# Six adaLN steps to a batch instead of four, from the 24th step on

## The chip, the core and the metric

One NeuronCore of a Trainium2 chip runs the whole program in one launch. The metric is device time in microseconds (us) of one execution; the kernel before was run three times. Engines are named as in the profile: PE (TensorE matmul), DVE (VectorE), ACT (ScalarE), POOL (GpSimd), SP (SyncE, which here issues nearly all loads). A profiled execution's times count from the start of its span.

## The reference

One decoder layer of width 2048 over 256 prompt tokens and 8 samples of 4 tokens (288 columns in all), in float32:

```python
mod = jax.nn.silu(c) @ w_ada + b_ada
sh1, sc1, g1, sh2, sc2, g2 = jnp.split(mod[:, None, :], 6, axis=-1)
h = layer_norm(x) * (1 + sc1) + sh1
z = (h @ w_in).astype(f32)
...
mix = jnp.concatenate([ya, yb], axis=-1).astype(x.dtype) @ w_out
x1 = layer_norm(ALPHA * x + g1 * mix, ln1_g, ln1_b)
h2 = layer_norm(x1) * (1 + sc2) + sh2
a, u = jnp.split(h2 @ w_up, 2, axis=-1)
...
ff = (jax.nn.gelu(conv, approximate=False) * u) @ w_down
x2 = layer_norm(ALPHA * x1 + g2 * ff, ln2_g, ln2_b)
```

Between z and mix lie an mLSTM of 4 heads (ya) and an HGRN2 of 8 heads (yb), both in chunks and with states that are returned. The change touches only when the product silu(c) @ w_ada ("adaLN", 2048 by 12288) is done; c has 9 rows (one for the prompt, eight for the samples).

## The kernel before

**Main products.** Activations stand as tiles of 128 features by 288 tokens. A weight "granule" is a tile of 128x1024 (512 KB): eight blocks of 128x128. SP loads it into `raw` (L220), ACT rounds it to `whi` (L229), DVE subtracts to `wlo` (L156); the activation is split in the same way. Per block PE runs three matmuls, hi by xh, hi by xl, lo by xh, so a granule is 24 matmuls. `raw` and `wlo` share NR=7 buffers, `whi` has NH=4; `granule()` asks for loads NQ=5 ahead, casts 3 ahead and subtractions 2 ahead. `project` takes two granules for one output tile in the PSUM pool "mm" and calls `slot()` after each.

**What fills the gaps.** `slot()` first runs one step of each background generator (`tick`), then adds `rate` to `credit` and calls `ada_batch`, then runs one step of each active generator (`mlstm`, `hgrn`, which use the PSUM pool "sd" of five buffers).

**adaLN.** w_ada is 192 steps of 512 KB. `ada_step(s)` first has SP issue the load of step s+6 (L306, NA=7 buffers `araw`), which waits until PE is done with step s-1; then PE multiplies `csp` (silu(c), 32 columns) by `araw[s]`, 8 matmuls of 128x256 into one PSUM tile `ad` (up to step 31 the tiles are narrower and the matmuls more). A unit is one such tile: seven small units, and then units of 16 steps, that end at steps 15, 31, 47, 63, 79, 95 and so on. When a unit ends, `ada_finish` transposes the tile on DVE (L345) and adds the bias into `mod`; a new unit that begins before that was ticked has the transpose issued first. There is one buffer "ad". In the start stage every other unit uses "sd" in its place; from the mixer on all use "ad" (`ad_tag`).

**What paces it.** In the start stage each granule's group adds 1 or 2 to `credit`; in the mixer `rate` is RATE=1.3 per slot. Before, four credits buy four steps. Steps 8 to 31 feed `h` (the first normalised activations), and `ad_stop` ends this pacing at step 172; the rest stands at fixed places in the tail.

**The entry of the mixer.** After the start's last slot SP issues the rest of the constants `cs`, the parameters `pks`, and the masks `lmf` (L579 to L582); `pks` is awaited by DVE for the HGRN bounds (`lbm`, `lbe`, `lb`).

Of the kernel before, what the change touches and what calls it, by code (L numbers as in the profile page):

```python
# [36 lines left out]
NR = 7  # L37
NQ = 5
NA = 7
BATCH = 4  # L40
NS = 4
RATE = 1.3
RA = 2
# [95 lines left out]
class K:  # L139
# [168 lines left out]

    def ada_batch(self):

        while self.credit >= BATCH:
            self.credit -= BATCH
            for _ in range(BATCH):
                self.ada_step()

    def ada_step(self):
# [1437 lines left out]
```

## Time and profile before

| | us |
|---|---|
| median of three runs | 1588.38 |
| lowest, highest | 1585.81, 1590.32 |
| the profiled execution | 1587.27 |
| its span | 1585.4 |
| PE busy in it | 1547.0 (98%) |
| DVE, ACT busy | 1033.2, 699.1 |

A line of a timeline gives start, duration (of a merged group), engine, source line, operation and shape; what stands in brackets is how long the engine was idle before it and what ended that. PEclk is TensorE's granted clock as a share of full speed, so 1.00 is 2.4 GHz and 0.50 is 1.2 GHz.

### The profile page before, as it was taken

To read this page: it belongs to the slowest core of one execution; us is meant where nothing else is said; L and a number is where in the kernel's file an instruction comes from. 1 tells how busy PE (TensorE), PEld (TensorE's weight loads), DVE (VectorE), ACT (ScalarE), POOL (GpSimd) and SP (SyncE) were. 2 spreads that over 40 slices of the span, in tenths; PEclk is the share of its full clock that TensorE was granted. 3 is DMA by queue.
4 is the path that set the end of the run, shared out by engine and by line. 5 is a ranking of instruction groups with operands and counts; after the bars stand their busy time and mean duration, and the time that the engine had idled before them with its cause. 6 is when DMAs were issued, how large, how long until landed. Compare 5 with 4: busy or idle time off the path is not lost.

```text
span 1585.4 us, 32088 instructions
## 1 busy us (share of the span) xinstructions
PE 1547.0 (98%) x12755; PEld 1456.8 (92%) x12755; DVE 1033.2 (65%) x2096; ACT 699.1 (44%) x1230; POOL 274.0 (17%) x429
## 2 busy tenths in 40 slices
PE   7999989999999989998999999999999999999998
PEld 5998988888888878886999999999999999999996
DVE  5766577878888788779755555455555555555554
ACT  4423234565656655335643433334343334444333
POOL 0000012344354343126311100011110001111000
PEclk9999999999999999999999999999999999999999
DMA  9998855777768678782555555555555555555551
GB/s 354 370 349 309 322 180 150 288 263 284 281 245 319 239 278 313 263 326 94 169 161 170 162 163 163 171 169 165 168 162 161 164 174 165 167 166 167 159 155 69
DMA packets 97542, 340.82 MB, mean 215 GB/s; under 512 B 11240, under 2 KB 15856, under 8 KB 96368
## 3 DMA queue, kind: packets, MB, share of 16 engines
q1 hardware_dynamic: 94896, 328.55, 60.8%
q0 software_dynamic: 2496, 10.22, 1.7%
q8 instruction: 101, 1.65, 0.4%
q14 instruction: 49, 0.40, 0.1%
HBM read 326.51 MB, written 12.21 MB: 214 GB/s over the span
## 4 chain that ended last, share of the span: by engine, by line
PE 86%; DVE 8%; ACT 3%; DMA 2%; issue 1%; SPq 0%; POOL 0%; ACTq 0%; DVEq 0%
PE mm L169 70%; PE sd L169 12%; PE ad L169 4%; DVE t L156 3%; DVE wlo L156 2%; ACT t L166 1%; DVE t L159 1%; ACT whi L229 1%; DVE c L159 1%; DMA raw<-w_in_b 1%; DMA raw<-w_out_b 0%; DMA pks<-pk 0%; DVE t L163 0%; DMA x<-xt 0%; ACT t L189 0%
## 5 line engine op out<-in xcount | busy, mean ns | idle before, releaser
L169 PE MATMUL mm<-t,whi 128*128 128x288 f32 (+1 forms) x4624 | 938.1, 298 | 14.0 <-ACT whi L229 5.8
L169 PEld LDWEIGHTS mm<-t,whi 128*128 128x128 f32 (+1 forms) x4624 | 741.6, 188 | 29.0 <-ACT whi L229 8.4
L169 PE MATMUL mm<-t,wlo 128*128 128x288 f32 x2312 | 683.4, 296 | 3.2 <-DVE wlo L156 3.2
L229 ACT CAST whi<-raw 128x1024 fp32r<-128x1024 f32 (+2 forms) x413 | 423.1, 1027 | 453.2 <-PE mm L169 223.8
L156 DVE TENSOR_TENSOR wlo<-raw,whi 128x1024 fp32r<-128x1024 f32 (+2 forms) x413 | 501.6, 1215 | 15.4 <-ACT whi L229 10.5
L169 PEld LDWEIGHTS mm<-t,wlo 128*128 128x128 f32 x2312 | 435.5, 188 | 4.1 <-DVE wlo L156 4.0
L169 PE MATMUL mm<-ff,whi 128*128 128x288 f32 x1376 | 276.1, 297 | 0.0
L169 PEld LDWEIGHTS mm<-ff,whi 128*128 128x128 f32 x1376 | 220.6, 188 | 2.5 <-issue 1.9
L166 ACT ACTIVATE t<-t 128x288 f32<-128x288 f32 (+4 forms) x317 | 121.5, 395 | 187.2 <-DVE t L156 130.4
L169 PE MATMUL mm<-ff,wlo 128*128 128x288 f32 x688 | 203.0, 295 | 0.0
L156 POOL TENSOR_TENSOR t<-t,t 128x288 f32<-128x288 f32 (+3 forms) x136 | 120.8, 896 | 168.6 <-ACT t L166 101.0
L159 DVE SCALAR_TENSOR_TENSOR t<-mm,mod,t 128x256 f32<-128x256 f32 x96 | 46.3, 482 | 148.1 <-PE mm L169 139.9
L169 PEld LDWEIGHTS mm<-ff,wlo 128*128 128x128 f32 x688 | 129.1, 188 | 0.0
L1558 POOL COPY convo<-ext 128x2 f32<-128x2 f32 x43 | 7.9, 184 | 629.4 <-ACT ext L1552 629.4
L156 DVE TENSOR_TENSOR t<-t,t 128x288 f32<-128x288 f32 (+4 forms) x203 | 89.8, 464 | 25.3 <-ACT t L189 21.2
L1553 DVE COPY ext<-mm 128x32 f32<-128x32 f32 x42 | 8.1, 192 | 138.8 <-ACT ext L1552 138.8
L169 PE MATMUL sd<-t,whi 128*128 128x288 f32 x464 | 95.0, 297 | 0.0
L169 PEld LDWEIGHTS sd<-t,whi 128*128 128x128 f32 x464 | 75.1, 190 | 0.0
L156 DVE TENSOR_TENSOR t<-cv,mm 128x256 f32<-128x256 f32 x80 | 20.7, 301 | 78.8 <-PE mm L169 78.8
L169 PE MATMUL ad<-araw,csp 128*32 128x256 f32 (+2 forms) x1312 | 68.4, 345 | 0.0
L169 PE MATMUL sd<-t,wlo 128*128 128x288 f32 x232 | 68.4, 296 | 0.0
L156 DVE TENSOR_TENSOR t<-t,mm 128x288 f32<-128x288 f32 x70 | 31.5, 451 | 54.5 <-PE mm L169 54.3
(259 smaller groups left out, 1206.8 us busy)
## 6 DMA issues: line engine op xcount, KB each, us to landing
araw<-w_ada SPq DMA_DIRECT2D x180, 512.0 KB, 5.7
raw<-w_up_b SPq DMA_DIRECT2D x160, 512.0 KB, 3.6
raw<-w_in_a SPq DMA_DIRECT2D x56, 512.0 KB, 7.3
raw<-w_in_b SPq DMA_DIRECT2D x56, 512.0 KB, 6.7
raw<-w_down SPq DMA_DIRECT2D x48, 512.0 KB, 3.5
raw<-w_down SPq DMA_DIRECT2D x32, 384.0 KB, 3.1
raw<-w_out_a SPq DMA_DIRECT2D x16, 512.0 KB, 6.2
raw<-w_out_b SPq DMA_DIRECT2D x16, 512.0 KB, 5.8
```

Of the source, the lines that this page charges most:

```text
L156: (eng or self.nc.vector).tensor_tensor(out=out, in0=a, in1=b, op=op)
L159: self.nc.vector.scalar_tensor_tensor(out=out, in0=a, scalar=s, in1=b, op0=op0, op1=op1)
L166: self.nc.scalar.activation(out, a, f, **kw)
L169: self.nc.tensor.matmul(out, lhsT, rhs, start=start, stop=stop, **kw)
L229: self.nc.scalar.copy(hi[:, :w], raw[:, :w])
L1553: nc.vector.tensor_copy(se[:, :, 2:6], self.smp(pa))
L1558: nc.gpsimd.tensor_copy(co[:, j, 0:2], ext[:, TP:TP + 2])
```

## The change

`BATCH` becomes 6, and from step 24 on a batch is taken when six credits have gathered; up to there it stays at four. The `while` becomes an `if`, so a call takes at most one batch. Buffers, rates and the steps' own instructions stay.

```diff
-BATCH = 4
+BATCH = 6
...
     def ada_batch(self):
 
-        while self.credit >= BATCH:
-            self.credit -= BATCH
-            for _ in range(BATCH):
+        n = BATCH if self.ad_n >= 24 else 4
+        if self.credit >= n:
+            self.credit -= n
+            for _ in range(n):
                 self.ada_step()
```

Each engine has as many instructions as before. In PE's order there were 52 runs of adaLN matmuls that stand together, and there are 40: steps 24 to 71 (start stage) go from 12 batches to 8, steps 72 to 171 (mixer) from 25 to 17, the last of which has four steps. From step 172 on nothing moves.

SP's queue at the entry of the mixer, where the last batch of the start stage (steps 66 to 71) asks for `araw`; then follow the next raw weight, `cs`, `pks` and `lmf`. Before:

```order
L220 DMA raw_2453<-w_in_a 128x1024
L220 DMA raw_2487<-w_in_a 128x1024
L306 DMA araw_2517<-w_ada 128x1024
L306 DMA araw_2523<-w_ada 128x1024
L306 DMA araw_2529<-w_ada 128x1024
L306 DMA araw_2535<-w_ada 128x1024
L220 DMA raw_2545<-w_in_a 128x1024
L579 DMA cs<-cst 128x416
L580 DMA pks<-pk 128x268
L582 DMA lmf<-lm 128x1008
```

The same place now:

```order
L220 DMA raw_2441<-w_in_a 128x1024
L220 DMA raw_2475<-w_in_a 128x1024
L306 DMA araw_2505<-w_ada 128x1024
L306 DMA araw_2511<-w_ada 128x1024
L306 DMA araw_2517<-w_ada 128x1024
L306 DMA araw_2523<-w_ada 128x1024
L306 DMA araw_2529<-w_ada 128x1024
L306 DMA araw_2535<-w_ada 128x1024
L220 DMA raw_2545<-w_in_a 128x1024
L580 DMA cs<-cst 128x416
L581 DMA pks<-pk 128x268
L583 DMA lmf<-lm 128x1008
```

Six loads of adaLN weights stand ahead of the raw weight and of `pks` where four stood.

DVE's queue in the mixer around step 112, where the unit of steps 96 to 111 ends (`a`, `t`, `s`, `stk` belong to the HGRN and mLSTM generators). Before:

```order
L156 TENSOR_TENSOR wlo_5531<-raw_5276,whi_5431 128x1024
L345 STREAM_TRANSPOSE adsb_5561<-ad_4805 128x256
L159 SCALAR_TENSOR_TENSOR mod<-adsb_5561,pks 128x72
L156 TENSOR_TENSOR t_5570<-t_5566,t_5569 128x288
L1028 COPY_PREDICATED a_5113<-lm,sd_5503 112x8x16
```

The transpose came one granule after the batch 108 to 111. Now the batch is 108 to 113 and the unit ends inside it; this is PE's order at it:

```order
L169 MATMUL mm_5506<-t_2398,whi_5431 128x288
L169 MATMUL mm_5506<-t_2399,whi_5431 128x288
L169 MATMUL mm_5506<-t_2398,wlo_5507 128x288
L169 MATMUL ad_4923<-araw_5203,csp 32x256 x4
L169 MATMUL ad_4923<-araw_5209,csp 32x256 x4
L169 MATMUL ad_4923<-araw_5215,csp 32x256 x4
L169 MATMUL ad_4923<-araw_5221,csp 32x256 x4
L169 MATMUL ad_5631<-araw_5227,csp 32x256 x4
L169 MATMUL ad_5631<-araw_5233,csp 32x256 x4
L169 MATMUL sd_5645<-t_5542,onesr 128x288
```

and this is DVE's:

```order
L156 TENSOR_TENSOR wlo_5572<-raw_5360,whi_5509 128x1024
L346 STREAM_TRANSPOSE adsb_5628<-ad_4923 128x256
L159 SCALAR_TENSOR_TENSOR mod<-adsb_5628,pks 128x72
L1029 COPY_PREDICATED a_5101<-lm,sd_5559 96x4x32
L156 TENSOR_TENSOR t_4985<-t_4985 128x128
L156 TENSOR_TENSOR t_5553<-t_5553,t_312 128x128
L159 SCALAR_TENSOR_TENSOR s_922_5164<-s_922_5164,eb_5160,sd_5557 128x128 x4
```

PE goes from the old unit's tile to the new one's in the one buffer "ad" between two neighbouring steps, and the transpose that frees it stands ahead of the HGRN work on DVE. The same holds at steps 128 (in the batch 126 to 131) and 160 (156 to 161). Step 80 (in 78 to 83) goes from "sd" to "ad". Step 32 lies in the batch 30 to 35, whose first unit ends after two steps and is the last that `h[6]` and `h[7]` need; the first matmuls that read them come right behind this batch, where before they came two granules later.

PE's order in the mixer at the batch 144 to 149. Now:

```order
L169 MATMUL mm_7610<-t_6181,wlo_7535 128x288
L169 MATMUL ad_7648<-araw_7268,csp 32x256 x4
L169 MATMUL ad_7648<-araw_7274,csp 32x256 x4
L169 MATMUL ad_7648<-araw_7280,csp 32x256 x4
L169 MATMUL ad_7648<-araw_7286,csp 32x256 x4
L169 MATMUL ad_7648<-araw_7292,csp 32x256 x4
L169 MATMUL ad_7648<-araw_7298,csp 32x256 x4
L780 MATMUL sd_7692<-cs,tri_7526 96x128
L169 MATMUL sd_7694<-t_7521 128x64 x2
L169 MATMUL mm_7711<-t_3700,whi_7537 128x288
```

Before:

```order
L169 MATMUL mm_7635<-t_6205,wlo_7560 128x288
L779 MATMUL sd_7680<-cs,tri_7551 96x128
L169 MATMUL sd_7682<-t_7546 128x64 x2
L169 MATMUL mm_7699<-t_3712,whi_7562 128x288
L169 MATMUL mm_7699<-t_3713,whi_7562 128x288
```

The new batch stands just ahead of the project `mm_7699` (now `mm_7711`); the batches of before stood a project ahead of it and a project behind it.

## Rows read from the trace of the kernel before

**Rows 1.** The page: busy time by engine, and the shares of the chain that ended last.

```profile
PE 1547.0 (98%) x12755; PEld 1456.8 (92%) x12755; DVE 1033.2 (65%) x2096; ACT 699.1 (44%) x1230; POOL 274.0 (17%) x429
...
PE 86%; DVE 8%; ACT 3%; DMA 2%; issue 1%; SPq 0%; POOL 0%; ACTq 0%; DVEq 0%
```

**Rows 2.** Waits of PE, by what ended them: total us, times, longest.

```profile
PE mm L169 <- ACT whi L229: 5.8, 2, 3.0
...
PE mm L169 <- DVE gt L156: 3.5, 2, 3.0
...
PE mm L169 <- DVE wlo L156: 3.2, 3, 1.7
```

**Rows 3.** Timeline of PE around a batch of four steps, and around a single step in the tail.

```profile
155.99 0.43 PE L169 MATMUL sd<-t,whi 128*128 128x288 f32 x2
156.25 0.29 PE L169 MATMUL sd<-t,wlo 128*128 128x288 f32 x1
156.47 1.93 PE L169 MATMUL ad<-araw,csp 128*32 128x256 f32 x32
158.34 0.53 PE L169 MATMUL mm<-t,whi 128*128 128x288 f32 x2
158.70 0.29 PE L169 MATMUL mm<-t,wlo 128*128 128x288 f32 x1
...
791.88 0.29 PE L169 MATMUL mm<-t,wlo 128*128 128x288 f32 x1
792.11 0.64 PE L169 MATMUL ad<-araw,csp 128*32 128x256 f32 x8
792.67 0.54 PE L169 MATMUL mm<-t,whi 128*128 128x288 f32 x2
793.05 0.29 PE L169 MATMUL mm<-t,wlo 128*128 128x288 f32 x1
```

**Rows 4.** Entry of the mixer: timelines of SP, DVE and PE, and the chain of waits (its line has start, us, what).

```profile
191.91 1.28 SPq L306 DMA_DIRECT2D araw<-w_ada  x3
...
194.31 6.93 DMA pks<-pk
...
201.26 0.17 DVE L156 TENSOR_TENSOR lbm<-pks 128x8 f32<-128x8 f32 x1 [5.84 <-DMA pks<-pk]
203.51 2.35 DVE L156 TENSOR_TENSOR wlo<-raw,whi 128x1024 fp32r<-128x1024 f32 x2
...
204.78 0.40 PE L169 MATMUL mm<-t,wlo 128*128 128x288 f32 x1 [1.68 <-DVE wlo L156]
```

**Rows 5.** Five stretches: us, busy time of PE, PEld, DVE, ACT, POOL (and instructions), granted clock, DMA share, GB/s.

```profile
20.00:87.00 67.00, 64.10 (x889) 60.37 (x878) 51.94 (x122) 29.86 (x54) 0.00 (x0) 0.97 0.98 374
206.90:211.00 4.10, 3.44 (x13) 3.12 (x14) 0.79 (x3) 0.00 (x0) 0.00 (x0) 0.60 0.38 124
384.00:392.00 8.00, 7.54 (x86) 6.29 (x87) 4.91 (x14) 6.48 (x17) 3.11 (x7) 1.00 0.79 285
584.40:590.00 5.60, 5.57 (x40) 5.19 (x44) 4.20 (x11) 3.07 (x9) 2.54 (x3) 0.70 0.17 69
646.00:652.00 6.00, 5.19 (x37) 4.93 (x38) 5.35 (x34) 0.84 (x1) 0.59 (x1) 1.00 0.32 126
```

**Rows 6.** Timeline of DVE at step 32, from the transpose of the unit to the last subtraction for `h[7]`.

```profile
80.80 0.31 DVE L345 STREAM_TRANSPOSE adsb<-ad 128x128 f32<-128x128 f32 x1
83.11 0.82 DVE L156 TENSOR_TENSOR t<-t,t 128x288 fp32r<-128x288 f32 x2
```

**Rows 7.** Timelines at step 112: DVE, ACT and PE.

```profile
423.04 0.45 DVE L345 STREAM_TRANSPOSE adsb<-ad 128x256 f32<-128x256 f32 x1 [1.27 <-PE ad L169]
...
430.51 0.30 DVE L1028 COPY_PREDICATED a<-lm,sd 96x128 f32<-96x128 uint8 x1 [0.77 <-PE sd L169]
...
434.12 0.46 DVE L163 TENSOR_SCALAR t<-sd 128x288 f32<-128x288 f32 x1 [0.32 <-PE sd L169]
...
431.59 1.04 ACT L229 CAST whi<-raw 128x1024 fp32r<-128x1024 f32 x1
...
433.59 0.43 PE L169 MATMUL sd<-t,onesr 128*128 128x288 f32 x2
439.58 0.38 PE L169 MATMUL sd<-t 128*128 128x128 f32 x2
```

**Rows 8.** ACT's longest wait for a raw weight behind a batch in the mixer, and PE's wait that followed.

```profile
633.72 1.93 PE L169 MATMUL ad<-araw,csp 128*32 128x256 f32 x32
644.36 1.05 ACT L229 CAST whi<-raw 128x1024 fp32r<-128x1024 f32 x1 [2.68 <-DMA raw<-w_out_b]
646.73 0.38 PE L169 MATMUL sd<-kd,ones 128*128 128x1 f32 x2 [1.44 <-DVE kd L1369]
```

**Rows 9.** Timelines of PE and DVE around the longest wait of PE for DVE, and an earlier wait of PE for DVE (384.46).

```profile
384.46 0.85 PE L169 MATMUL sd<-s,qm 128*32 128x128 f32 x16 [1.38 <-DVE a L1030]
569.85 1.93 PE L169 MATMUL ad<-araw,csp 128*32 128x256 f32 x32
580.90 0.56 PE L169 MATMUL sd<-t 128*128 128x64 f32 x4
583.70 0.48 DVE L159 SCALAR_TENSOR_TENSOR t<-mm,mod,t 128x256 f32<-128x256 f32 x1 [1.17 <-ACT t L639]
584.43 0.50 PE L169 MATMUL mm<-t,whi 128*128 128x288 f32 x2 [2.97 <-DVE gt L156]
```

## The prediction

> **What bounds the kernel now.** I read the page first, then the waits of PE, then the timelines at the places that the change moves. PE is busy 98% of the span and the chain that ended last runs 86% through PE, 8% through DVE [rows 1]. So a microsecond taken from PE's own work counts nearly in full, except in the stretches where the chain goes over DVE, ACT or DMA. PE's waits are few and single: 3.5 us in two for `gt`, 5.8 us in two for `whi`, 3.2 us in three for `wlo` [rows 2]. The second thing to see is what a batch costs PE, the third is what stands around the batches: weight loads on SP, the transpose on DVE, and the one buffer "ad".
>
> A difference of 0.3%, 4.8 us, is about what a measurement of this kernel can tell from no change.
>
> **What it removes.** From the last matmul before a batch of four to the first of the batch pass 156.47 - 156.25 = 0.22 us, where ordinary neighbours stand 0.13 apart (two in 156.25 - 155.99 = 0.26); from the first of the batch to the next ordinary one 158.34 - 156.47 = 1.87; and the next two take 158.70 - 158.34 = 0.36 in place of 0.26. Around the single step the middle one is 792.67 - 792.11 = 0.56 [rows 3]. Three more steps therefore cost 1.31, 0.437 each, and what is paid once for a batch is (0.56 - 0.437) + 0.09 + 0.10 = 0.31 to 0.33 us. The order has 52 batches before and 40 now: 12 x 0.33 = **-4.0 us**. The steps themselves stay. As the chain leaves PE for 14% of its length [rows 1], 14% of this goes to waits that only grow: **+0.5**.
>
> **What it moves, place by place.**
>
> Entry of the mixer. DVE stands 5.84 us for `pks`, then does the bounds and two subtractions, and PE waits 1.68 us for the first of these; the chain of waits goes over the load of `pks`, 6.93 us [rows 4]. Two more loads of 512 KB now stand ahead of it in SP's queue. In the start stage the queues bring 374 GB/s at a DMA share of 0.98 [rows 5], 1.40 us for a load, so `pks` comes 2.8 us later after the batch's start; PE's batch is two steps longer, 0.87. PE's wait grows by **+1.9**, from 1.68 to about 3.6. Bounds: 0, if the ring has room between the loads for the small `pks`, to +2.8. The fall of the clock behind this wait (0.60 from 206.9 to 211 [rows 5]) is there already and stays. The loads are late for nobody else: of the first mixer steps none runs before 270 us.
>
> Step 32. From the transpose to the last subtraction for `h[7]` DVE takes 83.11 + 0.82 - 80.80 = 3.13 us [rows 6]. Before, two granules lay between. Now PE has as cover the remaining four steps, 4 x 0.437 = 1.75, and the six matmuls of the group that read `h[4]` and `h[5]`, 0.8: **+0.6**, bounds 0 and +1.8 (one 1.2 us subtraction ahead of it on DVE).
>
> The one buffer. At steps 112, 128 and 160 PE's next step waits for the transpose of the tile that it has just filled. The transpose of such a tile takes 0.45 us, and DVE follows PE's last step within 0.1 when it is free, as at 423.04 where it waited for `ad` [rows 7]. With the way back I take 0.6 each, three times: **+1.8**; the lower end is 1.35 (the bare transposes), the upper 1.2 us more at each if DVE is in a subtraction, 5.4. At step 80 the tile goes to another buffer: nothing.
>
> DVE behind the transpose. A DVE instruction waits at its place in the queue, so what stands behind the transpose waits with it until PE has come to the end of the unit. At step 112 these are the HGRN operations that began at 430.51 before; now the batch begins when PE is through with the project, 433.59, its four steps end 1.75 later and the transpose and `mod` take 0.7: 436.0, 5.5 us late. Behind them ACT's cast of 431.59 and the copy of `sd` at 434.12 that frees a PSUM buffer are as late, or a microsecond later for the detour over ACT: 440.7. PE needs that buffer for the matmuls of 439.58, now 439.58 + 2.95 for the batch + 0.6 = 443.1 [rows 7]. It fits by some 2 us, with the next buffer of the pool by under 1. I take **+1.0** for all three places; bounds 0 and +4.
>
> Weights behind more loads. A batch of six puts 1.40 x 2 = 2.8 us more of loads ahead of the next raw weights, and gains 0.87 of that back, at two thirds as many places. The row that shows the price is the worst: behind the batch at 633.72 ACT waited 2.68 us for a raw weight, and PE 1.44 later on [rows 8]; that place has no batch just ahead of it any more. I take **+0.6**, between -1.4 (this wait goes) and +3.
>
> Where batches cover waits. PE's longest wait for DVE, 2.97 us for `gt` at 584.43, comes after a project and a few small matmuls from 580.90 on [rows 9], with a batch at 569.85 and the next only after it [rows 9]. Now the batch 144 to 149 stands right ahead of it, and none at 569.85: PE comes to the place 4 steps earlier and leaves the batch 2 steps later than before. If `gt`, which goes by a project of before and ACT (583.70) [rows 9], comes earlier with PE, the wait shrinks to nearly nothing, -2.7; if its time is fixed, by 0.5. Behind the wait the clock is 0.70 for 5.6 us [rows 5], (1 - 0.70) x 5.6 = 1.7 us, which goes too if the wait gets short. I take **-1.7**, between 0 and -4.4.
>
> **Sum**: -4.0 + 0.5 + 1.9 + 0.6 + 1.8 + 1.0 + 0.6 - 1.7 = +0.7 us. On the profiled execution, 1587.27, that gives 1588.0; on the median of the runs, 1.1 higher, 1589.1. I take **1588.5**: no difference that can be seen, with gains and losses of 4 to 6 us that cancel.
>
> **Rivals.**
>
> *The saving alone.* The moved work is hidden everywhere (DVE is busy 65% of the span [rows 1]), the wait at 584 goes with its clock, and only the wait at the entry and the three bare transposes remain: -4.0 - 4.4 + 1.9 + 1.4 = -5.1, some 1583. For it: PE's waits are few. Against it: PE takes three transposes uncovered, and the two places with the worst margins are new ones.
>
> *DVE's queue behind the transpose, slower.* The same mechanism as above with less slack: 5.5 us late, and the slack of PE's next use only 3. Each of the three places then costs 2.5 us, 7.5 in place of the 1.0 in the sum: +7.2, 1595. It decides from the point where the generators' PSUM buffers come free later than PE's next round of them, at step 112 some 7 us behind the transpose. For it: the pool "sd" has only five buffers, and both generators draw on it. Against it: the place that I worked through fits, and DVE has a third of its time free to catch up [rows 1].
>
> *The clock falls at the new waits, slower.* The fall costs 1.7 us wherever the trace shows it (0.60 from 206.9, 0.70 from 584.4). If each of the three new waits for the buffer does that, +5.1, together with the sum +5.8: 1593 to 1594. Rows speak against it: behind PE's waits of 1.38 us at 384.46 and 1.44 at 646.73 the granted clock is 1.00, the high level of 2.4 GHz [rows 5, 8, 9], and these are longer than 0.6. It would need 2.97 or a wait like the 1.68 with another soon behind it. The Trainium skill, TensorE: Matmul & The Clock Gate, section "A second HAM failure mode: psum-queue depth-cycling", says that short idles between matmul groups that cycle through PSUM buffers can make the clock swing and cost the return to full speed each time; by that, this rival would be the forecast, and the two rows with 1.00 are why it is not.
>
> *It does nothing of what it says.* The order excludes most of that; what is left is that a batch's fixed cost is not a cost, since the matmuls around it could catch up: then -4.0 and +0.5 drop out, and the rest gives +4.2, 1592.
>
> **How the numbers follow.** Forecast (within 4.8 us of before): 0.64. The saving alone: 0.15, of which nearly all lies past the bound. DVE's queue: 0.13, slower. The clock: 0.04, slower. No saving: 0.04, within the bound. So faster 0.15, same 0.68, slower 0.17. The range: at the low end the saving rival, 1583; at the high end the unknown costs of the forecast together (transposes and the queue at some 2 us over what I took each, the raw weights at 1), 1594, which takes in the clock and the edge of the queue rival.
>
> **What would show it.** Right: batches of 32 + 16 matmuls take 1.87 + 0.87 = 2.74 us to the next matmul; PE waits about 3.6 us for `wlo` near 206; three new waits of PE for DVE's transpose of 0.5 to 0.7 us; the wait for `gt` near 584 shorter. Wrong: a batch of six that takes more than 3 us without a wait (no fixed cost), a wait near 206 that has not grown (then the loads don't queue as I think), DVE idle on `ad` for over 2 us with PE waiting for an "sd" buffer after it, or new waits for `raw` on ACT. It is wrong above all if one of these stalls is over 3 us, since the clock would then go with it.

## The result, and the profile after

The changed kernel takes 1597.7 us (median of six runs, 1594.4 to 1600.92) against 1586.7 for the kernel before on the same chips: ratio 1.0072, 95% interval 1.006 to 1.0083. It is slower by 11 us, outside the range of the prediction. Its profiled execution took 1595.72 us, near the low end of its runs, so the trace shows 8.4 us of the 11.

The page, busy time by engine and the chain that ended last, as [rows 1]:

```profile
PE 1547.6 (97%) x12755; PEld 1457.6 (91%) x12755; DVE 1032.5 (65%) x2096; ACT 699.7 (44%) x1230; POOL 273.1 (17%) x429
...
PE 78%; DVE 13%; ACT 4%; DMA 3%; issue 2%; POOL 0%; SPq 0%; ACTq 0%; DVEq 0%; POOLq 0%
```

PE's busy time is what it was, not 4 us less; its waits have grown. The chain leaves PE for 22% of its length, where it left it for 14%, and most of that went to DVE.

The timeline of PE around a batch of six, as [rows 3]:

```profile
154.75 0.29 PE L169 MATMUL sd<-t,wlo 128*128 128x288 f32 x1
154.98 2.80 PE L169 MATMUL ad<-araw,csp 128*32 128x256 f32 x48
157.70 0.53 PE L169 MATMUL mm<-t,whi 128*128 128x288 f32 x2
158.07 0.29 PE L169 MATMUL mm<-t,wlo 128*128 128x288 f32 x1
```

157.70 - 154.98 = 2.72 us to the next matmul, as worked out (1.87 + 0.87). One batch costs what was forecast; whether twelve fixed costs are saved in sum, the busy time does not show. I took the matmuls that are not adaLN, which are as many in both programs and nearly in the same order, and compared when the 1100th (just ahead of the mixer's entry), the 1200th (behind it) and the 4500th (the mixer's last), counted from 0, start: 196.87, 215.1 and 717.4 us before, 196.54, 217.2 and 726.6 after. The start stage ends 0.3 us earlier, the entry takes 2.4 longer, the mixer 7.2 longer, and from there to the last matmul the distance stays at 9.2 to 9.3 (what follows that is 1.0 shorter).

The entry of the mixer, timelines of DVE and PE, as [rows 4]:

```profile
202.16 0.17 DVE L156 TENSOR_TENSOR lbm<-pks 128x8 f32<-128x8 f32 x1 [7.07 <-DMA pks<-pk]
204.42 2.35 DVE L156 TENSOR_TENSOR wlo<-raw,whi 128x1024 fp32r<-128x1024 f32 x2
...
205.69 0.61 PE L169 MATMUL mm<-t,wlo 128*128 128x288 f32 x1 [2.92 <-DVE wlo L156]
```

The wait is 2.92 us where it was 1.68.

The place of step 160, where the unit ends inside the batch 156 to 161: timelines of PE, DVE and POOL in the mixer.

```profile
633.60 1.93 PE L169 MATMUL ad<-araw,csp 128*32 128x256 f32 x32
636.10 1.07 PE L169 MATMUL ad<-araw,csp 128*32 128x256 f32 x16 [0.57 <-DVE adsb L346]
...
635.60 0.45 DVE L346 STREAM_TRANSPOSE adsb<-ad 128x256 f32<-128x256 f32 x1 [2.23 <-PE ad L169]
636.60 0.60 DVE L159 SCALAR_TENSOR_TENSOR s<-s,eb,sd 128x128 f32<-128x128 f32 x2
...
637.72 2.69 POOL L156 TENSOR_TENSOR t<-t,t 128x288 f32<-128x288 f32 x2 [7.59 <-DVE s L159]
...
643.14 0.44 PE L1122 MATMUL sd<-cs,t 128*128 128x128 f32 x2 [2.38 <-POOL t L156]
```

Read it from below: PE stood 2.38 us for POOL, POOL had waited for DVE's update of the HGRN state `s`, and DVE had stood 2.23 us idle with the transpose at the head of its queue until PE reached the end of the unit. PE's own wait for the transpose is the 0.57 above. How long DVE is held does not set the price. At step 112 it is held longest, and PE's wait for POOL behind it is the shorter one:

```profile
436.46 0.45 DVE L346 STREAM_TRANSPOSE adsb<-ad 128x256 f32<-128x256 f32 x1 [5.80 <-PE ad L169]
...
449.07 0.44 PE L1122 MATMUL sd<-cs,t 128*128 128x128 f32 x2 [0.71 <-POOL t L156]
```

The waits of DVE for `ad` and of ACT for raw weights, and of PE for DVE and POOL, from 220 to 720 us (total, times, longest):

```profile
DVE adsb L346 <- PE ad L169: 10.9, 5, 5.8
...
ACT whi L229 <- DMA raw<-w_in_b: 6.3, 3, 3.0
ACT whi L229 <- DMA raw<-w_out_b: 5.7, 4, 4.6
...
PE mm L169 <- DVE gt L156: 5.1, 4, 1.9
PE sd L1122 <- POOL t L156: 3.1, 2, 2.4
PE sd L169 <- DVE t L156: 2.0, 2, 1.6
PE ad L169 <- DVE adsb L346: 1.7, 3, 0.6
```

The same stretch before:

```profile
DVE adsb L345 <- PE ad L169: 1.9, 2, 1.3
...
ACT whi L229 <- DMA raw<-w_out_b: 6.6, 2, 3.9
ACT whi L229 <- DMA raw<-w_in_b: 1.4, 2, 1.0
```

The long wait of [rows 9] for `gt` has become shorter, 0.70 with 0.73 for `qm` behind it, and others have come: in all PE now waits 5.1 us for `gt`, in four places, where it waited 3.5 in two [rows 2].

```profile
278.14 0.40 PE L169 MATMUL sd<-t,onesr 128*128 128x288 f32 x1 [1.65 <-DVE t L156]
...
576.40 0.50 PE L169 MATMUL mm<-t,whi 128*128 128x288 f32 x2 [0.70 <-DVE gt L156]
580.53 0.85 PE L169 MATMUL sd<-s,qm 128*32 128x128 f32 x16 [0.73 <-DVE qm L156]
595.36 0.50 PE L169 MATMUL mm<-t,whi 128*128 128x288 f32 x2 [1.94 <-DVE gt L156]
672.55 0.50 PE L169 MATMUL mm<-t,whi 128*128 128x288 f32 x2 [1.38 <-DVE gt L156]
```

### The profile page after: what moved, and what is told of

The parts are those of the page before. It is cut to its first block, busy times and chain, and to the rows that moved or that the text cites. A ratio compares the mean times of both kernels' runs of the same rounds, so it can differ in the third digit from the quotient of the medians.

```text
span 1593.6 us, 32078 instructions
## 1 busy us (share of the span) xinstructions
PE 1547.6 (97%) x12755; PEld 1457.6 (91%) x12755; DVE 1032.5 (65%) x2096; ACT 699.7 (44%) x1230; POOL 273.1 (17%) x429
## 4 chain that ended last, share of the span: by engine, by line
PE 78%; DVE 13%; ACT 4%; DMA 3%; issue 2%; POOL 0%; SPq 0%; ACTq 0%; DVEq 0%; POOLq 0%
PE mm L169 65%; PE sd L169 9%; DVE t L156 4%; PE ad L169 3%; DVE wlo L156 3%; DVE t L159 2%; ACT t L166 2%; ACT whi L229 1%; DVE c L159 1%; DVE t L163 1%; DMA raw<-w_in_b 1%; DMA raw<-w_in_a 1%; DMA pks<-pk 1%; DMA raw<-w_out_a 0%; DVE s L159 0%
## 5 line engine op out<-in xcount | busy, mean ns | idle before, releaser
L169 PEld LDWEIGHTS mm<-t,whi 128*128 128x128 f32 (+1 forms) x4624 | 740.9, 188 | 29.7 <-issue 11.4
```

Of the source, the lines that this page charges most:

```text
L169: self.nc.tensor.matmul(out, lhsT, rhs, start=start, stop=stop, **kw)
```

## The experiments

Theories: A, the DVE queue held behind a transpose inside a batch; B, that 17 wide batches cover fewer waits than 25 narrow ones; C, that what counts is in which slots batches stand; D, that a batch's loads hold SP's queue. Times are medians in us; ratios, with their 95% intervals, are to the kernel before on the same chip, and differences in us are the ratio's excess times 1586; "mixer" is the time from the 1200th to the 4500th matmul in the one profiled execution, 502.2 us before and 509.4 after.

**Which stage.** The bound of n in `ada_batch` alone is changed.

```diff
-        n = BATCH if self.ad_n >= 24 else 4
+        n = BATCH if 24 <= self.ad_n < 72 else 4
```

> Six-step batches for steps 24 to 71 alone; the mixer keeps batches of four. Two theories of the 11 us. A (queue): unit ends inside a batch in the mixer (steps 80, 112, 128, 160) hold DVE's queue behind the transpose, some 7 to 8 us; the late pks at the mixer's entry is 2 to 2.5. B (cover): batches in the mixer are filler for PE while DVE catches up, and 17 wide ones cover less than 25 narrow ones, wherever units end. Neither differs here: no batch of the mixer is changed, so both expect the entry's wait alone, 2 to 3 us over the kernel before, less up to 1.3 of saved fixed cost: +1 to +3 us. More than +5 would mean that the start stage itself, or the later phase of the mixer's batches, is the larger part.

Measured: 1591.81, ratio 1.0035 (1.0021 to 1.0048), +5.6 us. That is more than expected. The mixer is as before, 502.0, and the entry, from the 1100th to the 1200th matmul, takes 23.6 us in the profiled execution. The granted clock there is the third number from the right (us, busy times of PE, PEld, DVE, ACT, POOL, clock, DMA share, GB/s). With sixes in the start stage only:

```profile
205.00:220.00 15.00, 13.00 (x57) 12.33 (x58) 7.34 (x14) 2.27 (x4) 1.94 (x5) 0.56 0.25 74
```

In the changed kernel:

```profile
205.00:220.00 15.00, 13.13 (x76) 12.46 (x77) 9.15 (x17) 4.72 (x8) 1.81 (x5) 0.77 0.30 87
```

In the kernel before:

```profile
205.00:220.00 15.00, 13.81 (x91) 13.26 (x91) 10.23 (x20) 5.55 (x8) 0.91 (x3) 0.89 0.39 122
```

The wait was 3.53 us in this run, and the clock then stood near its low level, 1.2 GHz, for most of the 15 us: (0.89 - 0.56) x 15 = 5 us more lost than before.

The 0.89 of the kernel before is not its usual value. Five of the kernels below have its order up to and through the entry (sixes in the mixer only, fours one and two slots later, fours with later loads, twos). PE waits 0.95 to 1.51 us for `wlo` in them, the clock stays up, and the entry takes 16.1 to 16.7 us, against 18.2. With sixes in the mixer only:

```profile
205.00:220.00 15.00, 13.23 (x96) 12.82 (x97) 11.70 (x24) 5.55 (x8) 0.00 (x0) 1.00 0.46 135
```

All six executions with sixes in the start stage and late `pks` have the fall: 0.54 to 0.77, the entry 20.3 to 24.4 us.

> Batches of four up to step 71, six from step 72 on. Here the units still end inside batches. A and B both expect most of the 11 us without the entry's part: +6 to +9 over the kernel before, and PE's wait for wlo at the mixer's entry back at 1.7 us. If it is below +4, the entry and the start stage carry more than both say.

Measured: 1594.18, 1.0049 (1.0034 to 1.0065), +7.8 us. Here the condition is `self.ad_n >= 72`. That is within what both theories expected; the wait for `wlo` is 1.15. The two stages add up to somewhat more than the whole, by no more than the intervals leave open.

The mixer has the order of the changed kernel here, and yet it takes 513.7 us. The whole mixers of this run and of the changed kernel:

```profile
211.90:725.60 513.70, 494.10 (x4167) 437.97 (x4165) 402.43 (x980) 268.60 (x622) 176.47 (x231) 0.99 0.73 260
217.20:726.60 509.40, 488.34 (x4166) 432.27 (x4165) 402.59 (x980) 268.96 (x622) 175.49 (x231) 1.00 0.74 262
```

The difference is the clock: 0.54 from 273 to 280, 0.72 from 592 to 598 and 0.57 from 641 to 645 lose 6.6 us by (1 - clock) x length, and the changed kernel's execution loses nothing. So two single mixers of the same order can differ by 4 us, and a smaller difference of two mixers below shows little by itself.

**The parameters first.** `cs` and `pks` are issued in the start stage, ahead of the loads of step 66 (68 with fours), and no longer behind those of the last batch.

```diff
         self.ad_n += 1
+        if s == 66:
+            a, b = CC["cap"][0], PK["b_ada"][1]
+            self.nc.sync.dma_start(self.cs[:, a:], self.i["cst"][:, a:])
+            self.nc.sync.dma_start(self.pks[:, b:], self.i["pk"][:, b:])
         self.ada_load(s + NA)
```

> The changed kernel with the loads of cs and pks issued ahead of the last six-step batch of the start stage. A and B both expect the wait for wlo at the mixer's entry, 2.9 us in the changed kernel, to fall to under 0.5 and the clock to stay up there: 3 to 5 us faster than the changed kernel (with the clock's 1.7), 1593 to 1595. If the total stays where it was while the wait is gone, the time is given back in DVE's stretch that follows.

Measured: 1591.74, 1.004 (1.0025 to 1.0055); from 1.0072, 5 us less. The wait is gone and the clock from 205 to 220 is 1.00. The same cure in the kernel before:

> The kernel before, with the loads of cs and pks issued ahead of the last batch of the start stage. The wait of 1.7 us for wlo at the mixer's entry and the clock's fall behind it (0.60 over 4 us) should go: -2 to -3.5 us. By cover or position some of that comes back where DVE is the bound behind it (260 to 300 us): -1 to -2.

Measured: 1583.34, 0.9988 (0.998 to 0.9997), -1.9 us, as expected.

**Unit ends.** First by narrower batches, then with every other batch left in its slot.

```diff
         n = BATCH if self.ad_n >= 24 else 4
+        if 24 <= self.ad_n < len(STEPS_ADA):
+            u = STEPS_ADA[self.ad_n][0]
+            n = min(n, sum(1 for v, _ in STEPS_ADA[self.ad_n:] if v == u))
```

> Batches of six from step 24 on, but never over the end of a unit: 6, 6, 4 of every 16 steps. It keeps 43 batches, three over the changed kernel. A expects the 7 to 8 us of the held DVE queue back, so within 3 us of the kernel before, and no wait of PE for the transpose; B expects most of the loss to stay, +6 or more, since the batches are as wide and nearly as far apart as in the changed kernel.

Measured: 1594.23, 1.005 (1.0036 to 1.0063), +7.9 us; mixer 507.8. By the time B is right: 3.5 us came back, and most of the loss stayed. PE waits for no transpose in the mixer, as A expected, but new waits of 2.0 and 2.1 us for `w` have come at 377 and 473.6. Slots moved here too, so this run does not decide.

```diff
+        n = self.ad_rest or (BATCH if self.ad_n >= 24 else 4)
+        if self.ad_rest or self.credit >= n:
+            self.credit -= 0 if self.ad_rest else n
+            self.ad_rest = 0
+            for k in range(n):
                 self.ada_step()
+                if k + 1 < n and 72 <= self.ad_n < self.ad_stop and STEPS_ADA[self.ad_n][1] == 0:
+                    self.ad_rest = n - 1 - k
+                    break
```

> The changed kernel, but in the mixer a batch stops where its unit ends (steps 80, 112, 128, 160) and takes the rest in the next slot. All other batches stand where they stood, so this is the held DVE queue and PE's wait for the transpose alone. A (queue) expects 4 to 7 us back from the changed kernel, less four more fixed costs of 0.33 us; B (cover) and C (position, below) expect at most the three waits of 0.6 us, less the same 1.3: no difference. The run with aligned batches gave back 3 us of 11, in which positions moved as well.

Measured: 1595.17, 1.0067 (1.0055 to 1.008): by the times not to be told from the changed kernel, as B and C expected. The trace shows a gain and what stands against it. The mixer takes 506.0, 3.4 us less although it pays four more fixed costs; the waits of DVE for `ad` fall from 10.9 to 2.9 us, and the five waits of PE named above (three of 0.57 for the transpose, 2.38 and 0.71 for POOL, 4.8 us in all) are gone. But this execution's clock at the entry is 0.57 from 205 to 220, and ACT waits for raw weights 12.7 us in all, behind which PE stands 2.2 us for `kd`:

```profile
DVE adsb L350 <- PE ad L169: 2.9, 3, 1.9
...
ACT whi L229 <- DMA raw<-w_out_b: 7.7, 3, 4.7
ACT whi L229 <- DMA raw<-w_in_b: 5.0, 2, 2.8
...
PE sd L169 <- DVE kd L1375: 2.2, 1, 2.2
```

So the held queue is a cost, by this trace about 3.4 + 1.3 = 4.7 us with the three bare waits (1.3 for four fixed costs), but not the only one, and cured alone it does not show in the times.

**Slots.** Fours, begun later in the mixer (2.6 and 3.9 for two and three slots).

```diff
             self.rate = RATE
+            self.credit -= 1.3
```

> The kernel before with every batch of four in the mixer one slot later (its credit starts 1.3 lower); nothing else. A third theory, C (position): which waits of PE for DVE, ACT and POOL a batch happens to cover is a matter of which slot it stands in, and the order of before was a good one; the width of the batch doesn't matter. C expects a loss like that of the aligned sixes in the mixer, +3 to +7 us; B (cover by width and distance) expects as many waits covered as before, within 2 us; A expects no change.

Measured: 1592.22, 1.0041 (1.0027 to 1.0055), +6.5 us; mixer 508.6. C expected that, A and B did not. Nothing was changed but the slot, and waits appear where the changed kernel has them; those for `gt` grow from 3.5 to 8.4 us:

```profile
273.29 0.61 PE L169 MATMUL sd<-t,onesr 128*128 128x288 f32 x1 [1.66 <-DVE t L156]
...
585.38 0.50 PE L169 MATMUL mm<-t,whi 128*128 128x288 f32 x2 [2.74 <-DVE gt L156]
591.08 0.50 PE L169 MATMUL mm<-t,whi 128*128 128x288 f32 x2 [1.95 <-DVE gt L156]
...
636.54 0.44 PE L1122 MATMUL sd<-cs,t 128*128 128x128 f32 x2 [1.36 <-POOL t L156]
```

> The same, two slots later. C expects a loss of a size of its own, 0 to +8 us, and other waits in the trace; B and A expect within 2 us of the kernel before.

Measured: 1587.67, 1.0017 (1.0008 to 1.0026), +2.7 us: another size than one slot later, as C has it, though the interval reaches down to the 2 us of the others.

> The kernel before with cs and pks first, and the mixer's batches of four three slots later. Three slots are 3.9 of the four credits that a batch needs, so from the second batch on they stand in nearly the slots of the kernel before, while the steps in each and the unit ends move by one batch. C expects nearly the time of the kernel before with pks first, -2 to +1 us; if it were the steps' loads or the unit ends that decide, it would be off by as much as one slot later was, +4 or more.

Measured (with `pks` first): 1584.04, 0.9991 (0.9982 to 1.0), as C expected: back in nearly the old slots, nearly the old time.

**Sixes in other slots**, with fours up to step 71 and `pks` first.

> Start stage as in the kernel before, cs and pks ahead of its last batch (worth -2 us by itself), and in the mixer batches of six that begin one slot later than the changed kernel's. With the changed kernel's own slots this would be 7.8 - 2 = +5.8 us over the kernel before (mixer-only run less the early pks). C (position): the sum depends on the slots alone, so some start slot gives a value near or under the kernel before, 1581 to 1590, and the spread over the start slots is 5 us or more. B (width): all start slots give about +4 to +7. C expects here anything from -3 to +8, B +4 to +7.

> The same, two slots later. C: -3 to +8 and different from the run before by some us; B: +4 to +7.

> The same, three slots later. C: -3 to +8 and different from the two before; B: +4 to +7.

Measured: 1599.33, 1602.56 and 1597.63, ratios 1.0087, 1.0104 and 1.0078: +14, +16 and +12 us. Neither theory had that. Much of it is the clock. The mixer two slots later:

```profile
210.50:733.40 522.90, 497.75 (x4167) 441.79 (x4166) 402.43 (x981) 269.80 (x622) 175.23 (x231) 0.98 0.71 255
```

In stretches with a clock of 0.51 to 0.66 the three mixers lose 5, 12 and 10 us by (1 - clock) x length, where the kernel before loses 1.7. Without that they take some 511, 511 and 508 us, close to the changed kernel's 509.4: among the slots tried none is good for sixes. That speaks for B, but all have unit ends inside their batches. The longest waits are not DVE's alone; three slots later PE waits for the load of an HGRN state, issued by SP behind the batches' loads:

```profile
386.63 1.50 PE L169 MATMUL sd<-s,qm 128*32 128x128 f32 x16 [5.67 <-DMA s<-s]
```

**The loads.** What a batch in the mixer loads is issued in the next slot, and not before each step.

```diff
     def slot(self):
 
+        self.ada_load(self.ad_want)
         self.tick()
...
-        self.ada_load(s + NA)
+        self.ad_want = s + NA
+        self.ada_load(s + 1 if 72 <= s < 172 else s + NA)
```

> The changed kernel, but the loads that a batch in the mixer asks for are issued together in the next slot, when PE has done or nearly done the steps that free their buffers, so SP does not stand before them. D expects most of the mixer's part back, 4 to 7 us under the changed kernel, and SP's waits for PE's adaLN matmuls nearly gone. B and C expect within 2 us of the changed kernel.

Measured: 1598.25, 1.0071 (1.0057 to 1.0085): no gain, against D. In the profiled execution the mixer takes 508.0, 1.4 us less, which is no more than two executions of one order differ by; SP's waits for PE with adaLN loads fall from 120.9 to 41.4 us from 220 to 720, ACT's waits for raw weights fall from 12.0 to 3.5 us, and the held DVE queue is still there (11.8 us of waits for `ad`).

> The same for the kernel before. D expects a gain too, 0 to 4 us; B and C within 1.5 us of the kernel before.

Measured: 1582.95, 0.9974 (0.9963 to 0.9985), -4.1 us: D for fours. ACT's waits for raw weights fall from 8.0 to 2.0 us.

**Width.** The batches of six split over two slots (as in the run that leaves the rest of a batch to the next slot, with the condition `k == 3 and n == BATCH`), and twos (`n = 2 if 72 <= self.ad_n < 172 else BATCH`, with BATCH = 4).

> The changed kernel, but every six of the mixer is four in its slot and two in the next. B (width) expects a gain although the fixed cost is paid 16 times more (+5.3 us): the waits of PE fall by more than 5 us, so not slower than the changed kernel. C and D expect the fixed cost to show, +3 to +6 over the changed kernel, unless the second slots happen to be good ones.

Measured: 1597.14, 1.0064 (1.0051 to 1.0076). No slower than the changed kernel with 16 more fixed costs, as B expected; PE stands idle 16.1 us of the mixer against 21.1. But the split also takes two of the unit ends out, so this is not B alone.

> The kernel before, with batches of two in the mixer (about every 1.5 slots). Fixed cost +8.4 us. B expects part of it back, since nearly every second slot then has cover: +2 to +6 over the kernel before, with PE's waits in the mixer under those of before. C expects +5 to +12, with other waits but no fewer.

Measured: 1589.88, 1.0015 (1.0006 to 1.0024), +2.4 us, as B expected, with fixed costs of 8.4. These stand in PE's busy time, so its idle time has to be compared: 10.0 us of the mixer, against 12.8 before and 21.1 after. Narrow batches leave less of it.

**All cures together.**

> The changed kernel with cs and pks ahead of the last batch of the start stage, the rest of a batch behind a unit's end in the next slot, and the mixer's adaLN loads a slot later. If the causes with names were all, the saved fixed costs would show: 1582 to 1585, under the kernel before. If width and slots hold what is left, it stays over it: 1587 to 1591.

Measured: 1583.02, 0.9981 (0.9972 to 0.999), -3.0 us: sixes with `pks` first, no unit end inside a batch of the mixer, and the loads a slot later are faster than the kernel before, the first of the two outcomes named. But the kernel before has none of the cures; the run after this one gives them to it. Mixer 503.0. Waits from 220 to 720 us:

```profile
DVE adsb L356 <- PE ad L169: 3.4, 4, 1.9
...
ACT whi L229 <- DMA raw<-w_out_b: 1.9, 3, 1.0
...
PE mm L169 <- DVE gt L156: 4.5, 4, 2.0
PE sd L169 <- DVE t L156: 2.0, 2, 1.6
```

> The kernel before with cs and pks first and the mixer's adaLN loads a slot later. Alone they gave -2 and -4 us; they act at different places, so -4 to -6 together: 1580 to 1583. Less than -4 would mean that both had shortened the same wait.

Measured: 1581.59, 0.9969 (0.9957 to 0.9981), -4.9 us, mixer 500.2. This is the best of all versions, and it has fours: 1.4 us under the sixes with all cures on the same chip (their runs 1581.62 to 1585.29, these 1581.04 to 1582.68).

## Why the prediction was wrong

*What it removes*: the price of a batch was right, 2.72 us for six steps, and the twos pay it: 25 batches more, and PE is busy 495.5 us of the mixer against 489.5 before, of which 1.7 by a low clock, so 0.31 for each. That the twelve batches fewer save 4.0 is not shown. PE's busy time is 1547.6 against 1547.0; in the mixer it is 488.3 after and 489.5 - 1.7 = 487.8 before. And the start stage does not end earlier with four batches fewer: its 1100th matmul starts at 195.6 to 197.8 us in the eight kernels with sixes there and at 195.4 to 196.9 in the twelve with fours, in a stage whose DMA share is 0.98 from 20 to 87 us [rows 5]. The rival *It does nothing of what it says* fits this better than the -4.0. Why the saving does not appear stays open.

*Entry of the mixer*: the mechanism and the growth of the wait were right (2.92 us here, 2.64 to 4.61 in the five executions with these loads, forecast 3.6), and one sentence was wrong: "The fall of the clock behind this wait ... is there already and stays." With the order of before the clock fell in one execution of six; with sixes in the start stage it fell in all six, to 0.54 to 0.77 over 15 us. The stage alone costs 5.6 us, and `pks` first gives 5 back (1.9 with fours), where I had +1.9.

*Step 32*: small, as forecast. PE has no wait over 0.3 us there.

*The one buffer*: right, three waits of 0.57 us, 1.7 in all. The clock does not fall behind them (1.00 from 434 to 440, 506 to 512 and 633 to 639 us), so that rival fell in the form that it had. The 2.4 us wait for POOL behind step 160 is another matter. Four executions have this mixer order. Behind this wait the clock stays up in the changed kernel's (1.00 from 643 to 648) and with the loads moved, and it falls in the other two: 0.57 from 641 to 645 with sixes in the mixer only, 0.57 from 637 to 641 with `pks` first. "It would need 2.97 or a wait like the 1.68 with another soon behind it" asked for too much.

*DVE behind the transpose*: the mechanism was right and stood among the rivals, its price was too low. With the bare waits it is 4.7 us by the trace, 3.0 without, against 1.0; inside its bound of +4. Step 112, which I had worked out, came as forecast (DVE held 5.80 us, PE's wait 0.71). Step 160, which I had not, costs 2.38 and goes over POOL.

*Weights behind more loads*: with the loads moved alone the sixes gain nothing that the times show. With `pks` first, unit ends and loads cured together give 9.4 us (1.0040 to 0.9981). Unit ends alone gave 0.8, without `pks` first. What I had not seen is that the two hide each other: with one cured PE runs into the other. Not all of it is the change's, since fours gain by moved loads as well: 4.1 us alone, 3.0 with `pks` first (0.9988 to 0.9969).

*Where batches cover waits*: the step that failed in kind. I looked at the one long wait that the new order shortens, and took -1.7. It did shorten, and PE's waits for `gt` grew from 3.5 to 5.1 us in all, with 1.65 for `t` at 278. The order before keeps many waits short or out of its list of waits altogether. Fours moved by a slot and nothing else cost 6.5 us, which the trace of before does not show. That the batches of before cover these waits is my reading of it; that their slots matter is shown.

The sum by the times, with `pks` first on both sides, is then: 8.2 us between sixes (1.0040) and fours (0.9988). Unit ends and loads make 9.4 - 3.0 = 6.4 of it, where I had 1.8 + 1.0 + 0.6 = 3.4. The 1.9 left (0.9981 to 0.9969) stand against -4.0 + 0.5 - 1.7 = -5.2 in the forecast, and that is the largest error: neither the saving nor the better cover came. The entry adds 5.1 - 1.9 = 3.2 (forecast 1.9), 11.4 in all. Each of these differences is uncertain by some 2 to 3 us. How the 1.9 split between slots, width and a saving that may be there stays open: twos leave PE less idle than fours, and fours spread over 6 us with their slots.

## What to carry to other kernels

Work that is put between other work as filler pays for its place: before it is moved, list what would stand uncovered at the old places, since a wait that it hides is in no list. When batches are made wider, look at every queue in which a wait of theirs stands at the head (here DVE's transposes and SP's loads), cut batches where they would wait for themselves, and move the rest apart. A small load that starts a stage belongs ahead of the large ones that are wanted later.

## What the runs showed of the hardware

The clock's answer to a wait differs from run to run. Behind a wait of 1.65 us for `t` at the mixer's first batches the granted clock was 1.00 in the changed kernel,

```profile
278.00:283.00 5.00, 4.86 (x39) 4.32 (x43) 4.87 (x18) 2.71 (x7) 1.10 (x2) 1.00 0.45 167
```

and behind the same wait (1.66 us) it was 0.54 where sixes stand in the mixer only:

```profile
273.00:280.00 7.00, 7.00 (x30) 6.44 (x31) 6.84 (x23) 3.90 (x10) 2.85 (x5) 0.54 0.28 111
```

Between 190 and 720 us of the twenty profiled executions PE stood 76 times for 1.0 to 1.6 us, and the clock fell to its low level in one case, during the wait or within 2 us of its end; 46 times for 1.6 to 2.5 us, with 24 falls; and 19 times for longer, with 18. This is a count over versions of one kernel and no rule. It says that a wait of some 2 us can cost a few us more by the clock in one execution and nothing in the next, so that single traces of the same order differ by as much as many a term of the sum above.
